# Two-layer S5 and attention decoder on one core: sums of squares on TensorE column parts in layer 0, and new engines and step orders

## The chip, the cores and the metric

One core of a Trainium2 chip runs the whole program. The metric is device microseconds of one execution, lower is better. Engines are called as the profile calls them: PE (TensorE), DVE (VectorE), ACT (ScalarE), POOL (GpSimd), SP (the queue that issues the loads).

## The reference

The input is x (256 tokens by 1024) and 256 memory tokens. There are two layers. Cut to what matters:

```python
for l in range(2):
    h = rms_norm(x, ln_mix[l]); z = h @ w_in[l]
    u_self, q_mem = z[..., :768], z[..., 768:]
    if l == 0: self_out = s5_mixer(u_self, ...)      # scan over tokens, gelu, gate
    else:      self_out = causal attention of rope(u_self) with keys, values of rms_norm(x) @ w_kv
    mem_out = memory_attention(q_mem, mem, mem_norm[l], w_mem_kv[l])   # 4 heads
    x = x + concat([self_out, mem_out]) @ w_out[l]
    x = x + conv_ffn(x, ...)
return rms_norm(x, final_norm)

def rms_norm(x, gain):
    return x * rsqrt(mean(x * x, axis=-1) + 1e-6) * gain
```

What the change touches is the mean of x * x of the input and of the memory in layer 0, the operators of the S5 mixer, and the copies of keys for attention.

## The kernel before, in words

Activations lie with features on the 128 partitions and tokens along the free dimension. Weights stream from HBM through one SP queue in the order of use. The program has five stages, one behind the other: the mixer of layer 0 (about the first 170 us), its feed-forward part, the mixer of layer 1 (from about 360 to 480 us), its feed-forward part, and the final norm.

**Norms.** The scale of a token is not applied to the input of a projection but to its output. ACT squares x into four tiles of 128x512 (`squares`, L275). `sums` (L279) adds the four on POOL in three instructions (L280 to L282) and then lets PE add over partitions: four products, each with a 128x128 part of the sum as the stationary operand and a column of ones as the moving one (L286), so that the sum of token n lands on partition n. An f32 product shows as two instructions in the trace. `root` (L290) makes the reciprocal root with a few 128x2 DVE instructions (L293, L301 to L305) and one POOL power (L299). `spread` (L312) brings the result to all partitions through PE, and ACT copies it to `rb` (L1015). In layer 0 the steps are called rx1 (sums), rx2 (root), rx3 (spread and copy) for x, and rm0 (squares), rm1, rm2, rm3 for the memory.

**Mixer of layer 0.** Its order is written out by hand in the string ORDER (L43): each word is a step, and the instructions of PE, DVE and POOL keep the order of the steps up to the bar, while ACT and SP are ordered by the compiler's planner. Behind the bar the string only sets priorities, and the planner orders all engines. The steps: P (one half block of the input projection, 8 PE instructions at L866; `project`, L860), u (DVE product of a projection block with rb, L874, which is the first use of rb), U (places u for the scan, ACT or DVE, L883, L885), E (powers for the rotation, L782, on DVE at L642 or on POOL at L639), X (input operators, two products and two sums of 512 elements, L751), T and t (PE transposes of X at L775 and their copies), V (output operators, three instructions of 1024 elements, L808), l and L (local operator, PE products on 32-column parts at L834 and L838, ACT copies at L849), S (the states, four parts: PE products at L895, a rotation of six DVE instructions at L902 to L907, two scans at L910 and L911, eight DVE instructions at L916 to L925), Y (outputs: PE at L939 and L943, a copy yc at L949 or L951, transposes, a copy yT at L959 or L961), G (gelu), K and K1 (memory keys and values of layers 0 and 1: eight PE steps, then the product kT at L392 and the copies `stack_k`), q (memory queries), h (a head in four parts), p (a pair of heads), g and o (gate, output projection), z (residual). Tuples beside ORDER say which of these parts run on which engine: V_POOL, X_POOL, E_POOL, Y_ACT, EVAC_ACT.

**Key copies.** `stack_k` (L415) makes, for each half of 64 partitions, a rounded copy on ACT (L421), the same copy into the other half on POOL (L422) and the remainder by a subtraction (L423), on POOL for the memory keys. `stack_q` (L406) does likewise with one copy and one subtraction.

**Mixer of layer 1.** ORDER1 (L61) lists its steps; here the string only sets priorities for the planner. ST_DVE names the stacks whose subtraction runs on DVE.

Of the kernel before, what the change touches and what calls it, by code (L numbers as in the profile page):

```python
# [10 lines left out]
F32 = mybir.dt.float32  # L11
# [31 lines left out]
ORDER = """  # L43
P E0 P P E1 P P P rm0 E0 Xr0 rx1 P P P rx2 E0 rx3 E0 E1 P Xi0 u0 D0 P U0 T0 U0 P U0 t0 P E1 D2 Xr1 P U0 V0 B0 Xi1 S0
u1 V0 V0 l0 T1 Xi2 U1 S0 P U1 S0 l0 V2 V1 P V1 L0 V2 t1 K Xr2 B1 S0 L0 T2 U1 K u2 V1 rm1 U2 K U2 U1 L0 L0 Y0 B2 K U2
t2 U2 E1 S1 V2 l1 D1 l1 l1 l1 L1 rm2 L1 S1 rm3 S2 Y0 S1 S1 K L1 K S2 K S2 Y0 L1 S2 K K1 Y1 K G0 G0 | q Y2 Y2 h1 Y1 h2
Y1 h1 h3 h3 K1 K1 h0 Y2 h2 G1 h1 G2 h0 K1 K1 h0 K1 G1 h2 G2 h3 h1 h2 h0 K1 h3 K1 g g g g g p1 g0 g0 g g1 p0 g1 p1 K1
g2 p0 o o o o g2 o o o o z3 z2 z1 z0
"""
V_POOL = ((2, 2),)  # L50
X_POOL = ((2, 0),)
E_POOL = ((0, 3), (1, 0), (1, 1), (1, 2))
H_DVE = (0, 1, 2)
Y_ACT = (1,)
EVAC_ACT = (0, 2)
T_ACT = ((0, 0), (0, 1), (1, 1), (2, 0), (2, 1))
# [4 lines left out]
ORDER1 = """  # L61
x x x x I I I X r1 r2 I I I I r3 I X Q0 qm Q1 K K Q1 h0 K X h3 X h2 Q2 K h1 h0 K h2 h2 R0 h1 h2 v Q0 R1 v R0 h3 R1 v
h0 h3 h1 K Q2 h10 h7 h0 h1 h5 v R2 h4 h3 h5 h4 h4 h7 v v h8 h5 h4 h11 h6 h10 h9 v v p0 h6 e0 h9 h10 h6 R2 h13 h5 p1 h7
h8 h14 h8 h7 h8 h12 h6 p1 p0 e1 h10 h9 h12 O h11 p3 h13 h12 h12 h9 h15 h11 p3 h13 h14 h11 h15 h14 p4 p5 h13 h15 p2 p2
p5 p4 p6 O h14 O h15 p7 p6 p7 O z0 O O O O z3 z2 z1
"""
ST_DVE = (('k', 1), ('q', 0))
BANKS = 'aaarwa'
# [71 lines left out]
def _body(ctx, tc, a):  # L140
# [138 lines left out]
    def sums(ts, bk):  # L279
# [8 lines left out]
        return p  # L288

    def root(p):  # L290

        m = sm.tile([128, 2], F32, name="m")
        V.tensor_scalar(m, p[:, :2], 1.0 / D, EPS, op0=ALU.mult, op1=ALU.add)  # L293
        return newton(m, 2)
# [83 lines left out]
    def mem_kv(l, bk, mem, ks, new, vm):  # L378
# [13 lines left out]
        V.tensor_mul(kT, v2(pk), rb2(rbm))  # L392
        ks.extend(stack_k(kT, new, G))
        for t in range(2):
# [10 lines left out]

    def stack_q(src, new, eng):  # L406

        n = src.shape[1]
        t = [new([128, n, T], F32R, "qs") for _ in range(2)]
        for h in range(2):  # L410
            S.activation(t[h][HALF[h]], src[HALF[h]], AF.Copy)
            eng.tensor_sub(t[h][HALF[1 - h]], src[HALF[h]], t[h][HALF[h]].bitcast(F32))
        return t

    def stack_k(src, new, eng):  # L415

        n = src.shape[1]
        t = [new([128, n, T], F32R, "ks") for _ in range(4)]
        for h in range(2):
            G.memset(t[2 + h][HALF[1 - h]].bitcast(F32), 0.0)  # L420
            S.activation(t[h][HALF[h]], src[HALF[h]], AF.Copy)  # L421
            G.tensor_copy(t[h][HALF[1 - h]], src[HALF[h]])  # L422
            eng.tensor_sub(t[2 + h][HALF[h]], src[HALF[h]], t[h][HALF[h]].bitcast(F32))  # L423
        return t
# [170 lines left out]
    def layer0(pool, s5):  # L595
# [412 lines left out]
        def rx1():  # L1008
            d["px"] = sums(xsq, bw)

# [9 lines left out]
        def rm1():  # L1020
            d["pm"] = sums(d["sm"], ba)

# [34 lines left out]
        def q():  # L1057
            qm = sq([128, 2, T], name="qm")
            V.tensor_mul(qm, v2(acc[3]), rb2(rb))
            qs.extend(stack_q(qm, st, V))  # L1060

# [32 lines left out]
    def layer1(pool):  # L1094
# [33 lines left out]
        def mem_q():  # L1128
            t = sl([128, 2, T], name="qm")
            V.tensor_mul(t, v2(d["q"][3]), rb2(rb))  # L1130
            qm.extend(stack_q(t, st, V if "qm" in ST_DVE else G))

        def rope(name, b, stack, out):
# [9 lines left out]
            yield  # L1143
            out[b] = stack(t, st, V if (name, b) in ST_DVE else G)
            yield
# [138 lines left out]
```

## Time and profile before

| what | value |
|---|---|
| median of 3 runs | 671.42 us (670.06 to 672.51) |
| the profiled execution's own time | 671.97 us |
| its span | 670.2 us |
| mean granted clock of PE | 0.966 of full speed |
| chain that ended last, by engine | PE 76%, DVE 18%, ACT 2%, issue 2% |

The span lies 1.8 us under the execution's own time. In a timeline each row is a start, a length, an engine, a line and an operation; several equal ones in a row are merged (x3), and the length then runs from the first start to the last end. What stands in brackets is the idle time of the engine before it and what ended it. In a table of stretches each engine has its busy time and, in brackets, its instructions; PEclk is the granted clock, where 1.00 is 2.4 GHz and 0.50 is 1.2 GHz.

### The profile page before, as it was taken

To read this page: it belongs to the slowest core of one execution; us is meant where nothing else is said; L and a number is where in the kernel's file an instruction comes from. 1 tells how busy PE (TensorE), PEld (TensorE's weight loads), DVE (VectorE), ACT (ScalarE), POOL (GpSimd) and SP (SyncE) were. 2 spreads that over 40 slices of the span, in tenths; PEclk is the share of its full clock that TensorE was granted. 3 is DMA by queue.
4 is the path that set the end of the run, shared out by engine and by line. 5 is a ranking of instruction groups with operands and counts; after the bars stand their busy time and mean duration, and the time that the engine had idled before them with its cause. 6 is when DMAs were issued, how large, how long until landed. Compare 5 with 4: busy or idle time off the path is not lost.

```text
span 670.2 us, 12678 instructions
## 1 busy us (share of the span) xinstructions
PE 629.2 (94%) x4968; PEld 595.2 (89%) x4968; DVE 547.5 (82%) x1011; ACT 408.0 (61%) x746; POOL 103.7 (15%) x117
## 2 busy tenths in 40 slices
PE   6787597999999999999999998999999999999995
PEld 5676586899999999999999997879999999999984
DVE  7989899786699988787769799875479998888872
ACT  5597454675566556565548788774446665555641
POOL 4596303031200000000003226301200000000000
PEclk9799698899999999999999997999999999999998
DMA  8722313256457436455465142424345555555511
GB/s 301 253 96 63 104 48 119 95 190 220 155 191 251 169 117 236 157 205 188 149 237 173 65 166 99 150 73 165 109 138 189 193 183 186 186 188 189 189 33 63
DMA packets 43356, 105.24 MB, mean 157 GB/s; under 512 B 3744, under 2 KB 14240, under 8 KB 43296
## 3 DMA queue, kind: packets, MB, share of 16 engines
q1 hardware_dynamic: 42720, 103.84, 45.6%
q8 instruction: 39, 0.64, 0.4%
q10 hardware_dynamic: 576, 0.59, 0.3%
q14 instruction: 21, 0.17, 0.1%
HBM read 103.37 MB, written 1.05 MB: 156 GB/s over the span
## 4 chain that ended last, share of the span: by engine, by line
PE 76%; DVE 18%; ACT 2%; issue 2%; DMA 0%; POOL 0%; DVEq 0%; ACTq 0%
PE psU L262 13%; PE psU L260 12%; PE psU L261 12%; PE acc L562 9%; PE acc L261 7%; PE acc L262 7%; PE acc L260 7%; DVE wlo L119 2%; DVE X L642 1%; PE psO L481 1%; DVE xt L642 1%; PE ps L388 1%; DVE cf L649 1%; DVE Vd L642 1%; PE psT L465 1%
## 5 line engine op out<-in xcount | busy, mean ns | idle before, releaser
L115 ACT ACTIVATE whi<-wraw 128x1024 fp32r<-128x1024 f32 (+1 forms) x176 | 181.1, 1037 | 102.7 <-PE psU L261 52.0
L119 DVE TENSOR_TENSOR wlo<-wraw,whi 128x1024 fp32r<-128x1024 f32 (+1 forms) x176 | 212.8, 1212 | 31.2 <-PE psU L262 14.9
L262 PE MATMUL psU<-xhi,wlo 128*128 128x256 f32 x704 | 197.6, 281 | 1.1 <-DVE wlo L119 1.1
L260 PE MATMUL psU<-xhi,whi 128*128 128x256 f32 x704 | 198.0, 282 | 0.0
L261 PE MATMUL psU<-xlo,whi 128*128 128x256 f32 x704 | 197.4, 281 | 0.0
L262 PEld LDWEIGHTS psU<-xhi,wlo 128*128 128x128 f32 x704 | 133.2, 189 | 1.4 <-DVE wlo L119 1.3
L261 PEld LDWEIGHTS psU<-xlo,whi 128*128 128x128 f32 x704 | 132.6, 189 | 0.7
L260 PEld LDWEIGHTS psU<-xhi,whi 128*128 128x128 f32 x704 | 132.4, 188 | 0.7
L533 DVE SCALAR_TENSOR_TENSOR y<-u,held,y 128x254 f32<-128x254 f32 (+1 forms) x176 | 77.9, 477 | 1.5 <-ACT y L531 1.3
L531 ACT ACTIVATE y<-u,held 128x256 f32<-128x256 f32 x88 | 47.7, 590 | 20.6 <-DVE u L526 20.6
L526 DVE TENSOR_TENSOR u<-psU,rb 128x512 f32<-128x512 f32 x44 | 30.3, 688 | 33.3 <-PE psU L262 33.1
L261 PE MATMUL acc<-al,whi 128*128 128x256 f32 x176 | 49.6, 282 | 0.0
L260 PE MATMUL acc<-ah,whi 128*128 128x256 f32 x176 | 49.6, 282 | 0.0
L262 PE MATMUL acc<-ah,wlo 128*128 128x256 f32 x176 | 49.6, 282 | 0.0
L280 POOL TENSOR_TENSOR sq<-sq 128x512 f32<-128x512 f32 x5 | 8.2, 1648 | 229.7 <-ACT sq L275 229.7
L866 PE MATMUL acc<-xg,wraw 128*128 128x256 f32 x128 | 34.5, 431 | 5.5 <-ACT xg L856 5.5
L866 PEld LDWEIGHTS acc<-xg,wraw 128*128 128x128 f32 x128 | 27.8, 222 | 10.0 <-ACT xg L856 5.5
L262 PEld LDWEIGHTS acc<-ah,wlo 128*128 128x128 f32 x176 | 33.6, 191 | 0.0
L261 PEld LDWEIGHTS acc<-al,whi 128*128 128x128 f32 x176 | 33.6, 191 | 0.0
L260 PEld LDWEIGHTS acc<-ah,whi 128*128 128x128 f32 x176 | 33.5, 190 | 0.0
L262 PE MATMUL acc<-xhi,wlo 128*128 128x256 f32 x112 | 31.6, 283 | 0.0
L261 PE MATMUL acc<-xlo,whi 128*128 128x256 f32 x112 | 31.4, 281 | 0.0
(253 smaller groups left out, 1322.8 us busy)
## 6 DMA issues: line engine op xcount, KB each, us to landing
wraw<-w_up SPq DMA_DIRECT2D x88, 512.0 KB, 4.2
wraw<-w_down SPq DMA_DIRECT2D x44, 512.0 KB, 4.0
wraw<-w_out SPq DMA_DIRECT2D x16, 512.0 KB, 3.6
wraw<-w_in SPq DMA_DIRECT2D x15, 512.0 KB, 5.7
wraw<-w_mem_kv SPq DMA_DIRECT2D x8, 512.0 KB, 3.8
wraw<-w_kv SPq DMA_DIRECT2D x6, 512.0 KB, 7.4
wraw<-w_kv SPq DMA_DIRECT2D x8, 384.0 KB, 3.4
wraw<-w_glu SPq DMA_DIRECT2D x6, 384.0 KB, 3.7
```

Of the source, the lines that this page charges most:

```text
L115: self.nc.scalar.activation(hi[:, c], t[:, c], AF.Copy, scale=1.0 if g_ is None else g_)
L119: self.nc.vector.tensor_sub(lo[:, c], t[:, c], hi[:, c].bitcast(F32))
L260: PE.matmul(out, whi, ahi, start=first, stop=False, skip_group_check=True)
L261: PE.matmul(out, whi, alo, start=False, stop=False, skip_group_check=True)
L262: PE.matmul(out, wlo, ahi, start=False, stop=last, skip_group_check=True)
L280: G.tensor_add(ts[0], ts[0], ts[1])
L526: V.tensor_mul(u, v2(p), rb2(rb))
L531: S.activation(y[:, j], u[:, j], AF.Identity, bias=cp(3), scale=cp(2))
L533: V.scalar_tensor_tensor(y[:, j, d:], u[:, j, :T - d], cp(2 - d), y[:, j, d:], op0=ALU.mult, op1=ALU.add)
L562: PE.matmul(dacc[2 * t + h], a_, w_[:, 512 * i:512 * i + 512], start=False, stop=last and a_ is al, skip_group_check=True)
L642: V.tensor_tensor(o, a_, b_, op=op)
L866: PE.matmul(acc[2 * h + b][:, 256 * (m % 2):256 * (m % 2) + 256], w[:, 512 * i + 128 * m:512 * i + 128 * m + 128], xg[k // 2][:, k % 2], s ...
```

## The change

- `sums_pe` replaces `sums` at rx1 and rm1, both in layer 0. There is no addition on POOL; PE takes each of the four tiles of squares as stationary operand in parts of 32 columns, each on its own 32 columns of the array, and accumulates: 64 products with one moving column in place of four. The norms of the feed-forward parts and of layer 1 keep `sums`.
- V_POOL: the last sum of V2 goes from POOL to DVE. E_POOL: the second part of E0 goes from DVE to POOL, the first part of E1 from POOL to DVE.
- Y_ACT: yT of block 2 goes from DVE to ACT. EVAC_ACT: yc of block 1 goes to ACT and that of block 2 to DVE.
- CP_ACT: the second key copy of both memory stacks (names m0, m1) goes from POOL (L422) to ACT. The engines of all subtractions stay as they are; they only get other names.
- ORDER and ORDER1 list the same steps in another order.

```diff
@@ -41,30 +41,31 @@
 ENG = mybir.EngineType
 MANUAL = {ENG.PE, ENG.DVE, ENG.Pool}
 ORDER = """
-P E0 P P E1 P P P rm0 E0 Xr0 rx1 P P P rx2 E0 rx3 E0 E1 P Xi0 u0 D0 P U0 T0 U0 P U0 t0 P E1 D2 Xr1 P U0 V0 B0 Xi1 S0
-u1 V0 V0 l0 T1 Xi2 U1 S0 P U1 S0 l0 V2 V1 P V1 L0 V2 t1 K Xr2 B1 S0 L0 T2 U1 K u2 V1 rm1 U2 K U2 U1 L0 L0 Y0 B2 K U2
-t2 U2 E1 S1 V2 l1 D1 l1 l1 l1 L1 rm2 L1 S1 rm3 S2 Y0 S1 S1 K L1 K S2 K S2 Y0 L1 S2 K K1 Y1 K G0 G0 | q Y2 Y2 h1 Y1 h2
-Y1 h1 h3 h3 K1 K1 h0 Y2 h2 G1 h1 G2 h0 K1 K1 h0 K1 G1 h2 G2 h3 h1 h2 h0 K1 h3 K1 g g g g g p1 g0 g0 g g1 p0 g1 p1 K1
-g2 p0 o o o o g2 o o o o z3 z2 z1 z0
+P E0 rm0 E0 P P P Xr0 P P rx1 E1 E0 V0 P P P P rx2 P rx3 E0 D0 P u0 Xi0 U0 E1 t0 Xi1 V0 P B0 U0 E1 U0 P U0 T0 P u1 V1
+Xr1 S0 V0 T1 l0 V2 U1 S0 P V1 l0 V2 Xi2 K K L0 S0 Xr2 L0 u2 D1 U1 S0 L0 t1 L0 T2 U1 K U2 t2 rm1 U2 Y0 V2 B2 B1 U1 K V1
+D2 rm2 S1 Y0 U2 E1 l1 l1 l1 U2 S1 K l1 rm3 S2 K L1 S1 S2 L1 K L1 Y0 S1 K G0 S2 S2 K1 K L1 | Y1 Y2 q K1 K1 Y1 Y1 h2 h1
+K1 h1 G1 h3 K1 h3 h1 h1 G0 Y2 Y2 h2 G1 K1 G2 h2 K1 G2 g h0 h0 g h0 g h3 g h2 g0 h0 g h3 g1 p0 K1 g0 K1 o o g g2 g1 g2
+p0 o p1 o p1 o o z0 o o z1 z3 z2
 """
-V_POOL = ((2, 2),)
+V_POOL = ()
 X_POOL = ((2, 0),)
-E_POOL = ((0, 3), (1, 0), (1, 1), (1, 2))
+E_POOL = ((0, 1), (0, 3), (1, 1), (1, 2))
 H_DVE = (0, 1, 2)
-Y_ACT = (1,)
-EVAC_ACT = (0, 2)
+Y_ACT = (1, 2)
+EVAC_ACT = (0, 1)
 T_ACT = ((0, 0), (0, 1), (1, 1), (2, 0), (2, 1))
 U_ACT = ((1, 1, 1, 0), (1, 1, 1, 1), (1, 1, 1, 1))
 
 
 
 ORDER1 = """
-x x x x I I I X r1 r2 I I I I r3 I X Q0 qm Q1 K K Q1 h0 K X h3 X h2 Q2 K h1 h0 K h2 h2 R0 h1 h2 v Q0 R1 v R0 h3 R1 v
-h0 h3 h1 K Q2 h10 h7 h0 h1 h5 v R2 h4 h3 h5 h4 h4 h7 v v h8 h5 h4 h11 h6 h10 h9 v v p0 h6 e0 h9 h10 h6 R2 h13 h5 p1 h7
-h8 h14 h8 h7 h8 h12 h6 p1 p0 e1 h10 h9 h12 O h11 p3 h13 h12 h12 h9 h15 h11 p3 h13 h14 h11 h15 h14 p4 p5 h13 h15 p2 p2
-p5 p4 p6 O h14 O h15 p7 p6 p7 O z0 O O O O z3 z2 z1
+x x x x I I I X r1 r2 I I I I r3 I X Q0 qm K Q1 K Q1 Q2 h0 K X h3 X h2 K h1 h0 K h2 h2 R0 h1 h2 v Q0 R1 R0 h3 R1 v v
+h0 h3 h1 K Q2 h10 h7 h0 h1 h5 v R2 h4 h3 h5 h4 h4 h7 v v p0 h8 h5 h4 h11 h6 h10 v p0 h6 e0 h9 h10 h6 R2 h13 h8 h5 p1
+h7 h14 h9 v h8 h7 h8 h12 h6 p1 e1 h10 h9 h12 O h11 p3 h13 h12 h12 h9 h15 h11 p3 h13 h14 h11 h15 h14 p4 p5 h13 h15 p2
+p2 p5 p4 p6 O h14 O h15 p7 p6 p7 O O z0 O O O z3 z2 z1
 """
-ST_DVE = (('k', 1), ('q', 0))
+ST_DVE = ('k1', 'q0', 'w0')
+CP_ACT = ('m0', 'm1')
 BANKS = 'aaarwa'
 
 
@@ -287,6 +288,17 @@
                           start=(h == 0), stop=(h == 1))
         return p
 
+    def sums_pe(ts, bk):
+
+        p = bk()
+        for t in range(2):
+            for i, (q, h) in enumerate((q, h) for q in ts for h in range(2)):
+                for c in range(4):
+                    n = 256 * h + 128 * t + 32 * c
+                    PE.matmul(p[32 * c:32 * c + 32, t:t + 1], q[:, n:n + 32], ones, start=i == 0,
+                              stop=i == 2 * len(ts) - 1, tile_position=(0, 32 * c), skip_group_check=True)
+        return p
+
     def root(p):
 
         m = sm.tile([128, 2], F32, name="m")
@@ -390,7 +402,7 @@
             yield
         kT = sq([128, 2, NM], name="kT")
         V.tensor_mul(kT, v2(pk), rb2(rbm))
-        ks.extend(stack_k(kT, new, G))
+        ks.extend(stack_k(kT, new, f"m{l}"))
         for t in range(2):
             S.activation(vm[:, t], pv[:, 256 * t:256 * t + 256], AF.Copy, scale=rtok[:, t:t + 1])
         yield
@@ -403,24 +415,30 @@
     def values_of(v):
         return lambda h: [v[:, t, 64 * h:64 * h + 64] for t in range(2)]
 
-    def stack_q(src, new, eng):
+    def less(name, out, src, hi):
+        (V if name in ST_DVE else G).tensor_sub(out, src, hi.bitcast(F32))
+
+    def stack_q(src, new, name):
 
         n = src.shape[1]
         t = [new([128, n, T], F32R, "qs") for _ in range(2)]
         for h in range(2):
             S.activation(t[h][HALF[h]], src[HALF[h]], AF.Copy)
-            eng.tensor_sub(t[h][HALF[1 - h]], src[HALF[h]], t[h][HALF[h]].bitcast(F32))
+            less(name, t[h][HALF[1 - h]], src[HALF[h]], t[h][HALF[h]])
         return t
 
-    def stack_k(src, new, eng):
+    def stack_k(src, new, name):
 
         n = src.shape[1]
         t = [new([128, n, T], F32R, "ks") for _ in range(4)]
         for h in range(2):
             G.memset(t[2 + h][HALF[1 - h]].bitcast(F32), 0.0)
             S.activation(t[h][HALF[h]], src[HALF[h]], AF.Copy)
-            G.tensor_copy(t[h][HALF[1 - h]], src[HALF[h]])
-            eng.tensor_sub(t[2 + h][HALF[h]], src[HALF[h]], t[h][HALF[h]].bitcast(F32))
+            if name in CP_ACT:
+                S.activation(t[h][HALF[1 - h]], src[HALF[h]], AF.Copy)
+            else:
+                G.tensor_copy(t[h][HALF[1 - h]], src[HALF[h]])
+            less(name, t[2 + h][HALF[h]], src[HALF[h]], t[h][HALF[h]])
         return t
 
     def scores(bk, q, k, i, h, causal):
@@ -1006,7 +1024,7 @@
             gens[f"G{b}"] = gelu2(b)
 
         def rx1():
-            d["px"] = sums(xsq, bw)
+            d["px"] = sums_pe(xsq, bw)
 
         def rx2():
             d["yx"] = root(d["px"])
@@ -1018,7 +1036,7 @@
             d["sm"] = squares([m.rearrange("p a t -> p (a t)") for m in memT])
 
         def rm1():
-            d["pm"] = sums(d["sm"], ba)
+            d["pm"] = sums_pe(d["sm"], ba)
 
         def rm2():
             d["ym"] = root(d["pm"])
@@ -1057,7 +1075,7 @@
         def q():
             qm = sq([128, 2, T], name="qm")
             V.tensor_mul(qm, v2(acc[3]), rb2(rb))
-            qs.extend(stack_q(qm, st, V))
+            qs.extend(stack_q(qm, st, "w0"))
 
         calls = {"rx1": rx1, "rx2": rx2, "rx3": rx3, "rm0": rm0, "rm1": rm1, "rm2": rm2, "rm3": rm3, "q": q}
         for b in range(3):
@@ -1128,7 +1146,7 @@
         def mem_q():
             t = sl([128, 2, T], name="qm")
             V.tensor_mul(t, v2(d["q"][3]), rb2(rb))
-            qm.extend(stack_q(t, st, V if "qm" in ST_DVE else G))
+            qm.extend(stack_q(t, st, "w1"))
 
         def rope(name, b, stack, out):
             sw = sl([128, 2, T], name="sw")
@@ -1141,7 +1159,7 @@
             V.tensor_mul(sw, sw, rb2(ropeS))
             V.tensor_add(t, t, sw)
             yield
-            out[b] = stack(t, st, V if (name, b) in ST_DVE else G)
+            out[b] = stack(t, st, f"{name}{b}")
             yield
 
         def keys():
```

## Rows read from the trace of the kernel before

**Rows 1.** The page's part 1: busy time, share of the span, instructions.

```profile
PE 629.2 (94%) x4968; PEld 595.2 (89%) x4968; DVE 547.5 (82%) x1011; ACT 408.0 (61%) x746; POOL 103.7 (15%) x117
```

**Rows 2.** Busy time by stretch: columns PE, PEld, DVE, ACT, POOL, PEclk, DMA share, GB/s.

```profile
20.00:30.00 10.00, 8.14 (x29) 7.12 (x30) 8.84 (x41) 7.90 (x18) 2.56 (x4) 0.66 0.69 245
60.00:70.00 10.00, 3.26 (x20) 2.53 (x20) 10.00 (x9) 2.90 (x5) 4.32 (x3) 0.92 0.17 52
...
140.00:150.00 10.00, 10.00 (x83) 8.68 (x82) 8.02 (x12) 6.93 (x11) 5.40 (x4) 1.00 0.56 186
410.00:420.00 10.00, 8.98 (x40) 8.42 (x40) 9.32 (x19) 7.84 (x17) 3.73 (x3) 0.50 0.50 168
```

**Rows 3.** Timeline of POOL, first 110 us: start, length, instruction, [idle before].

```profile
17.91 1.29 POOL L280 TENSOR_TENSOR sq<-sq 128x512 f32<-128x512 f32 x1
...
55.93 1.49 POOL L280 TENSOR_TENSOR sq<-sq 128x512 f32<-128x512 f32 x1
...
66.91 2.35 POOL L639 TENSOR_TENSOR Vd<-Vd,vt 128x1024 f32<-128x1024 f32 x1 [5.68 <-DVE vt L642]
...
107.11 0.74 POOL L422 CAST ks<-kT 64x512 fp32r<-64x512 f32 x1 [25.41 <-DVE kT L392]
```

**Rows 4.** Timeline of DVE up to the first product with rb (L874).

```profile
17.99 1.25 DVE L746 TENSOR_TENSOR s5c<-cf 128x24 f32<-128x24 f32 x1
...
19.26 2.73 DVE L731 TENSOR_TENSOR ct<-s5c 128x48 f32<-128x48 f32 x4
...
22.82 0.64 DVE L731 TENSOR_TENSOR ct<-s5c 128x72 f32<-128x72 f32 x3
...
29.95 1.31 DVE L642 TENSOR_TENSOR xt<-s5c 128x512 f32<-128x512 f32 x2
31.30 2.04 DVE L642 TENSOR_TENSOR X<-xt 64x512 f32<-64x512 f32 x2
34.11 0.69 DVE L874 TENSOR_TENSOR uT<-acc,rb 128x512 f32<-128x512 f32 x1 [0.78 <-ACT rb L1015]
```

**Rows 5.** Timeline of PE: first sums, projection steps, local operator, first scores.

```profile
21.86 1.86 PE L286 MATMUL ps<-held,sq 128*128 128x1 f32 x8 [3.35 <-POOL sq L282]
23.58 7.29 PE L866 MATMUL acc<-xg,wraw 128*128 128x256 f32 x24
...
31.16 3.62 PE L866 MATMUL acc<-xg,wraw 128*128 128x256 f32 x16
...
47.05 0.43 PE L834 MATMUL ps<-Vd,Bz 128*32 128x64 f32 x16 [2.73 <-DVE Vd L642]
...
113.45 0.77 PE L431 MATMUL psS<-ks,qs 128*128 128x256 f32 x2 [3.03 <-DVE qs L412]
```

**Rows 6.** Timeline of ACT: the copy of rb.

```profile
33.70 0.38 ACT L1015 ACTIVATE rb<-ps 128x256 f32<-128x256 f32 x1
```

**Rows 7.** Timeline of DVE behind it, to the memory keys (L392).

```profile
48.37 0.69 DVE L780 COPY RT<-ps 128x512 f32<-128x512 f32 x1 [1.46 <-PE ps L775]
...
55.61 0.68 DVE L906 TENSOR_TENSOR rot<-rot 128x512 f32<-128x512 f32 x1
56.21 1.76 DVE L907 TENSOR_TENSOR rot<-rot 128x512 f32<-128x512 f32 x1
57.89 2.28 DVE L910 TENSOR_TENSOR_SCAN rot<-dec,rot 128x512 f32<-128x512 f32 x1
...
67.36 2.45 DVE L916 TENSOR_TENSOR rot<-rot,E 128x512 f32<-128x512 f32 x1
...
74.96 1.22 DVE L642 TENSOR_TENSOR Vd<-Vd,vt 128x1024 f32<-128x1024 f32 x1
...
82.75 0.69 DVE L902 TENSOR_TENSOR rot<-ps,E 128x512 f32<-128x512 f32 x1 [1.16 <-PE ps L895]
...
86.42 1.22 DVE L910 TENSOR_TENSOR_SCAN rot<-dec,rot 128x512 f32<-128x512 f32 x1
...
106.36 0.68 DVE L392 TENSOR_TENSOR kT<-ps,held 128x512 f32<-128x512 f32 x1
```

## The prediction

> **What bounds the kernel now.** I read the page's busy times first [rows 1]: PE is busy 94% of the span and DVE 82%, so most of the program is PE's, and only a stage where PE waits can give time back. The table of stretches says which stages these are [rows 2]. From 140 us on PE is full for as long as the mixer and the feed-forward part last; whatever moves the start of that stage moves the end one to one. Before it PE is short of work: 3.26 us of 10 between 60 and 70, while DVE has its full 10, and between 20 and 30 PE also runs at a granted clock of 0.66, a mean of its two levels. So the first 106 us, up to the product kT, are a DVE queue whose order is written by hand, and a change is worth there what it takes from that queue. In the mixer of layer 1 one stretch stands out, 410 to 420, where PE is busy for 8.98 us at half clock; little else is open there.
>
> The timelines of POOL and DVE, laid side by side, show where the queue loses time. While POOL adds squares [rows 3], DVE instructions on two SBUF operands take about one POOL instruction longer [rows 4, 7]: the 24-column L746 took 1.25 us, four L731 took 2.73 us where three later ones took 0.64, the scan L910 took 2.28 us at 57.89 and 1.22 at 86.42. This hold is the first thing the change removes.
>
> **Part by part, up to u0.** *rx1.* The PE timeline shows PE idle for 3.35 us ahead of the four old products [rows 5], waiting for POOL's third addition; PE was thus free at 21.86 - 3.35 = 18.5. The new products need only the squares from ACT, so they start there. There are 64, or 128 instructions. Their price is not in the trace. The nearest row is L834, also 32 stationary columns on a column part, 16 instructions in 0.43 us, 27 ns each. The far bound is that a part costs what a whole product costs: L286, eight in 1.86 us at about half clock, 232 ns, so 116 ns at full clock. Below 27 ns I see no reason to go. I take 27, because width and part are the same, and keep 116 for the rivals: 128 x 27 ns = 3.45 us, until 22.0.
>
> The Trainium skill has a rule against it: "TensorE: Matmul & The Clock Gate", section "Wait — 56ns, not 53.3ns?", says that small products have floors of their own, about 25 ns from start to start, or about 62 ns where the sequencer's microcode handles each. The row of L834 agrees with the first floor. By the second, rx1 would last 7.9 us and the sum below would come out 4.5 us later.
>
> *rx3 and u0.* Between rx1 and rx3 the new order has five P steps where the old one had three. A step is 8 instructions, 3.62 / 16 x 8 = 1.81 us at full clock [rows 5], so 9.05 us. Behind its pause PE took 7.29 us for three steps instead of 5.43: 1.86 us lost to the clock. The pause goes; whether the clock falls during rx1 all the same, no row shows. Bounds 0 and 1.86; I take 0.9. So the spread starts at 22.0 + 9.05 + 0.9 = 31.9 and with 0.6 for it and 0.4 for ACT's copy u0 starts at 33.0 (32.0 to 34.0). Before it was 34.11 [rows 4]. The copy stood at 33.70 [rows 6] behind work that waited for Xi0; in the new order Xi0 comes behind u0, so nothing of it can stand ahead of the copy.
>
> *The wait that this makes.* DVE used to do Xi0 while rb was coming. In the new order nothing of DVE stands between rx2 and u0. DVE ended Xi0 at 31.30 + 2.04 = 33.34. Off that come the hold on L746 and L731 (1.25 - 0.21 and 2.73 - 4 x 0.21, together 2.9) and Xi0 itself (33.34 - 29.95 = 3.4); on come 1.2 for the first product of V0, which moves ahead. E0's second part leaves DVE and E1's first part comes to it, ten small instructions for eight; I cost the swap at nothing, within 0.3 us either way. DVE is ready at 28.3 and waits 4.7 us for rb, with the whole queue behind it. So the 2.9 us of rx are nearly all given back here, and u0 gains 1.1 us.
>
> **From u0 to kT.** Before, this was 106.36 - 34.11 = 72.25 us [rows 4, 7]. The terms:
> - rm1 without POOL: L907 took 1.76 us against 0.68 of L906, the scan 2.28 against 1.22, and I take the same again for the second scan: -3.2.
> - V2's sum to DVE: POOL's 2.35 us go, which held L916 for 2.45 instead of 0.68; the sum costs DVE 1.22, as V1's did: -1.77 + 1.22 = -0.55.
> - DVE's old idle, 1.46 ahead of RT and 1.16 ahead of L902: -2.6. The wait for POOL's power in rm2 stays.
> - Xi0 now lies behind u0, 1.31 + 2 x 0.68 = +2.7 without POOL beside it; V0's first product has left: -1.2.
> - rm1's 128 instructions on PE, 3.45 us, cost nothing as long as they run while PE waits for the states of block 0; that stretch had 6.7 us of idle PE in ten [rows 2].
> - New waits of DVE in the new order: U0, T1, S1 and S2 all come on PE shortly ahead of their use. At least 0, at most about 5, twice the old idle; I take 2.0.
> - Xr2 stays on POOL, but now falls beside more instructions on two SBUF operands. Between 0 and 3.5 (one hold of 1.06 to 1.77 for two or three more); I take 1.0.
>
> Sum: 72.25 - 3.2 - 0.55 - 2.6 + 2.7 - 1.2 + 2.0 + 1.0 = 70.4. kT starts at 33.0 + 70.4 = 103.4, 3.0 us earlier.
>
> **Behind kT.** Both POOL copies of the keys (0.74 us for the first [rows 3]) go to ACT, which then has six copies in line where it had four; POOL's subtractions come earlier, the queries' copies later. PE waited 3.03 us for the first scores [rows 5]. Between 0.7 lost and 1.5 won; I take 0.8. yT of block 2 leaves DVE, about 0.6 as for other 512-element copies [rows 7]; the swap of yc is one for one and costs nothing unless PE waits for it, 0.7 at most. Together 1.4. The second memory stack runs while PE is full and gives nothing.
>
> **Layer 1.** ORDER1 is only a priority for the planner, and no engine changes. All that is open is the half-clock stretch [rows 2], where full clock would give back up to 4.5 us; a worse order could make another such stretch. I take 0, within 2 either way.
>
> **Sum.** 3.0 + 1.4 = 4.4 us off the profiled execution's 671.97, so 667.6. That execution stands 0.55 above the median of the runs shown; against the median I forecast 667.0.
>
> **The rivals.**
> *More is won.* The stall at u0 is short because rx1 keeps PE's clock, the queue behind finds its PE results ready, and layer 1 gets back its half-clock stretch. Forecast less 1.0 (u0), 2.0 (waits), 2.5 of layer 1: about 661. For it: 2.9 + 3.2 + 1.77 us of holds are measured. Against it: the DVE wait at u0 is in the order itself. Chance 0.17.
> *No change.* Small products at the skill's second floor, or waits at their upper bound: by either, +4.5 or +3 and Xr2's +2.5, 670 to 672.5. For it: PE is idle for 6.7 us of one stretch of ten [rows 2] and the new order moves nearly every step, so a hold can come back as a wait for PE. Against it: 27 ns in the trace. Chance 0.18.
> *Slower: the column parts do not overlap.* All 64 products add to two columns, each part to the same place every fourth time; if one has to wait for another, rx1 takes up to 128 x 116 ns = 14.8 us, u0 starts at 44.4 and the end is 11.4 us later than forecast, 678.4. It decides from about 80 ns per instruction, 10.2 us for rx1, which is 6.7 more than I take and 2 us above the time before. For it: no row has one moving column on a column part. Against it: L834 accumulates too and shows 27 ns. Chance 0.12.
>
> **How the numbers follow.** The forecast has 0.53. Its own range, with u0 by 1 us, waits by 2.0 down and 3 up, Xr2, the keys and layer 1 at their bounds but not all at once, is 663 to 670. For 8 in 10 I reach to the middle of the two outer cases, 660 to 673. About 0.3%, 2 us, is what a measurement of this kernel can tell from no change. Faster by more (below 669.4): 0.17 and nearly all of 0.53, 0.67. Within it: 0.18. Slower: 0.15, the last rival and a part of the second.
>
> **What would show it.** In the new profile: no L280 on POOL in layer 0; L746 and L731 at some 0.2 us; L910 at 1.2 us each time; 128 short PE instructions from about 18.5 us, lasting some 3.5 us; an idle DVE of 3 to 6 us ahead of L874, ended by ACT's rb; kT at 102 to 104 us. The sum is wrong if u0 starts later than 36, if DVE is idle for more than 5 us between u0 and kT, or if the layer 1 mixer changes by over 2 us.

## The result, and the profile after

The changed kernel takes 660.56 us (median of 4 runs, 660.06 to 661.47) against 670.74 us for the kernel before (4 runs beside it, 669.62 to 672.51): a ratio of 0.9844, 95% interval 0.9819 to 0.9869. It is 10.2 us faster; the profiled span fell by 11.1, from 670.2 to 659.1. The forecast was 667.0 us, 4.4 us faster: the direction was right and the time lies in the range of 660 to 673, at its very end, but more than twice the forecast was won. The profile of the kernel before is of an execution of 671.97 us, 1.2 above this median, so the stretches below overstate the gain by about 1 us.

I cut both profiles at the same places: u0 (the first product with rb), kT, the first memory scores, the first product of the gate, the first sums over partitions of the feed-forward part of layer 0 (ffn0), the same of layer 1's mixer and feed-forward part, and the end of the span. Start times and differences in us:

| stretch | before | after | change | forecast |
|---|---|---|---|---|
| start to u0 | 34.11 | 30.96 | -3.15 | -1.1 |
| u0 to kT | 72.25 | 71.18 | -1.07 | -1.85 |
| kT to scores | 7.09 | 7.67 | +0.58 | |
| scores to gate | 10.66 | 3.86 | -6.80 | kT to gate: -1.4 |
| gate to ffn0 | 50.42 | 50.48 | +0.06 | 0 |
| ffn0 to sums of layer 1's mixer | 191.02 | 191.51 | +0.49 | 0 |
| these to sums of layer 1's feed-forward part | 112.85 | 113.01 | +0.16 | 0 |
| these to the end of the span | 191.80 | 190.43 | -1.37 | 0 |

The page of the kernel after (its first line and part 1) shows 5.3 us less PE time than [rows 1], at a mean granted clock of 0.980 for 0.966, and 11 us less on POOL:

```profile
span 659.1 us, 13141 instructions
PE 623.9 (95%) x5208; PEld 589.8 (89%) x5208; DVE 541.0 (82%) x1009; ACT 411.6 (62%) x751; POOL 92.4 (14%) x108
```

Stretches of the kernel after, with the columns of [rows 2]:

```profile
20.00:30.00 10.00, 8.36 (x41) 7.10 (x40) 8.01 (x32) 6.59 (x17) 4.76 (x14) 1.00 1.05 375
60.00:70.00 10.00, 8.74 (x199) 7.52 (x200) 9.86 (x14) 8.10 (x24) 0.00 (x0) 0.84 0.01 3
110.00:120.00 10.00, 10.00 (x71) 9.82 (x71) 8.48 (x21) 5.41 (x15) 0.00 (x0) 0.83 0.44 157
400.00:410.00 10.00, 8.02 (x38) 7.47 (x39) 9.32 (x17) 8.06 (x16) 4.22 (x3) 0.55 0.50 165
```

One of these stretches was not among the rows of before; there it reads:

```profile
110.00:120.00 10.00, 6.30 (x27) 5.61 (x27) 9.69 (x13) 6.30 (x13) 2.63 (x3) 0.64 0.55 197
```

PE keeps its full clock between 20 and 30 us, where it had 0.66, and between 110 and 120 it is busy all the time (at a granted clock of 0.83), where it was busy for 6.30 at 0.64. The slow stretch of layer 1's mixer is still there, only some 10 us earlier.

PE up to u0, to set beside [rows 5]:

```profile
17.58 1.27 PE L298 MATMUL ps<-held,sq 128*32 128x1 f32 x128
18.78 8.90 PE L884 MATMUL acc<-xg,wraw 128*128 128x256 f32 x40
29.33 0.71 PE L324 MATMUL ps<-held,y 128*128 128x128 f32 x4 [1.64 <-DVE y L317]
```

The 128 new instructions take 1.27 us, 10 ns each. The five P steps behind them take 8.90 us, 1.78 each (2.43 before). PE is ready for the spread at 27.7 and then waits for DVE's y. DVE in the same time and just behind, to set beside [rows 4]:

```profile
18.61 0.18 DVE L764 TENSOR_TENSOR s5c<-cf 128x24 f32<-128x24 f32 x1
...
18.84 0.56 DVE L749 TENSOR_TENSOR ct<-s5c 128x48 f32<-128x48 f32 x4
...
26.55 1.22 DVE L660 TENSOR_TENSOR Vd<-s5c 128x1024 f32<-128x1024 f32 x1
27.68 0.15 DVE L305 TENSOR_SCALAR m<-ps 128x2 f32<-128x2 f32 x1
28.66 0.16 DVE L313 TENSOR_TENSOR t<-y 128x2 f32<-128x2 f32 x1 [0.82 <-POOL y L311]
...
30.96 0.69 DVE L892 TENSOR_TENSOR uT<-acc,rb 128x512 f32<-128x512 f32 x1 [1.69 <-ACT rb L1033]
31.57 1.62 DVE L660 TENSOR_TENSOR xt<-s5c 128x512 f32<-128x512 f32 x2
```

L764 and L749 are L746 and L731 of before: 0.18 for 1.25 us and 0.56 for 2.73. The root (from L305) stands behind the first product of V0. Further down the same queue, to kT:

```profile
47.46 0.69 DVE L798 COPY RT<-ps 128x512 f32<-128x512 f32 x1 [0.42 <-PE ps L793]
...
51.60 1.51 DVE L924 TENSOR_TENSOR rot<-rot 128x512 f32<-128x512 f32 x1
53.03 1.76 DVE L925 TENSOR_TENSOR rot<-rot 128x512 f32<-128x512 f32 x1
...
59.73 1.23 DVE L928 TENSOR_TENSOR_SCAN rot<-dec,rot 128x512 f32<-128x512 f32 x1
...
98.44 0.68 DVE L996 TENSOR_TENSOR yl<-yT,yh 128x512 fp32r<-128x512 f32 x1
...
102.14 0.68 DVE L404 TENSOR_TENSOR kT<-ps,held 128x512 f32<-128x512 f32 x1
```

The scan takes 1.23 (L910 took 2.28), and between u0 and kT DVE waits only for 0.42 us for PE and 0.83 for POOL's power. L924 and L925 are held by Xr2 on POOL (1.51 and 1.76 for 0.68), whose second half is this row:

```profile
51.30 2.94 POOL L657 TENSOR_TENSOR X<-xt 64x512 f32<-64x512 f32 x2
```

L996 ends the gelu work of block 0, which now lies ahead of kT.

PE behind kT, first before (between these lines stand the scores of [rows 5]), then after:

```profile
107.13 3.29 PE L388 MATMUL ps<-wraw,memT 128*128 128x256 f32 x14
...
119.64 4.83 PE L388 MATMUL ps<-wraw,memT 128*128 128x256 f32 x14
124.11 0.47 PE L260 MATMUL acc<-yh,whi 128*128 128x256 f32 x1
```

```profile
104.14 1.13 PE L397 MATMUL ps<-memT,wraw 128*128 128x256 f32 x4
105.11 1.03 PE L400 MATMUL ps<-wraw,memT 128*128 128x256 f32 x4
109.81 0.39 PE L449 MATMUL psS<-ks,qs 128*128 128x256 f32 x1 [3.68 <-DVE qs L419]
...
113.67 0.56 PE L261 MATMUL acc<-yh,whi 128*128 128x256 f32 x1
```

Before, 28 instructions of K1's values (second memory projection) follow kT, 14 of them behind the scores and ahead of the gate. After, nine follow kT, eight of them in the two rows shown (each group of four is two products), and none the scores. Scores to gate lost 6.8 us: 4.5 are these 14 instructions (119.64 to 124.11), 0.9 a group of PE transposes that no longer stands there, 0.7 a wait for yc that is gone, and 0.7 faster scores. From kT to the gate that is 6.2 us, where I had forecast 1.4.

### The profile page after: what moved, and what is told of

Its sections match the earlier page's. It is cut to its first block, busy times and chain, and to the rows that moved or that the text cites. A ratio compares the mean times of both kernels' runs of the same rounds, so it can differ in the third digit from the quotient of the medians.

```text
span 659.1 us, 13141 instructions
## 1 busy us (share of the span) xinstructions
PE 623.9 (95%) x5208; PEld 589.8 (89%) x5208; DVE 541.0 (82%) x1009; ACT 411.6 (62%) x751; POOL 92.4 (14%) x108
## 4 chain that ended last, share of the span: by engine, by line
PE 75%; DVE 3%; ACT 1%; issue 1%; DVEq 0%; POOL 0%; POOLq 0%
PE psU L263 13%; PE psU L261 13%; PE psU L262 13%; PE acc L580 9%; PE acc L262 7%; PE acc L263 7%; PE acc L261 7%; PE psO L499 1%; DVE wlo L120 1%; PE psS L449 1%; PE psT L483 1%; PE psS L450 1%; PE acc L538 1%; PE acc L1181 1%; PE acc L1182 0%
## 5 line engine op out<-in xcount | busy, mean ns | idle before, releaser
L120 DVE TENSOR_TENSOR wlo<-wraw,whi 128x1024 fp32r<-128x1024 f32 (+1 forms) x176 | 216.7, 1234 | 16.7 <-PE acc L263 8.1
L281 POOL TENSOR_TENSOR sq<-sq 128x512 f32<-128x512 f32 x3 | 4.8, 1598 | 233.7 <-DMA wraw<-w_kv 178.1
L884 PE MATMUL acc<-xg,wraw 128*128 128x256 f32 x128 | 32.0, 411 | 5.6 <-ACT xg L874 5.6
L884 PEld LDWEIGHTS acc<-xg,wraw 128*128 128x128 f32 x128 | 26.0, 207 | 9.6 <-ACT xg L874 5.6
```

The source lines that it names most:

```text
L120: self.nc.vector.tensor_sub(lo[:, c], t[:, c], hi[:, c].bitcast(F32))
L884: PE.matmul(acc[2 * h + b][:, 256 * (m % 2):256 * (m % 2) + 256], w[:, 512 * i + 128 * m:512 * i + 128 * m + 128], xg[k // 2][:, k % 2], s ...
```

## The experiments

Theory: the gain is the end of POOL's hold on DVE, plus PE work that no longer stands behind the scores. Rivals: the new orders and engines bring it and the sums matter little; or DVE and PE had been waiting for the sums, and POOL's hold matters little. Times are medians; each ratio is to the kernel before on the same chip. Cuts are start times of one profile each.

| kernel | us | ratio (95%) | u0 | kT | scores | gate | ffn0 |
|---|---|---|---|---|---|---|---|
| old_plus_sums | 663.56 | 0.9898 (0.9878 to 0.9918) | 31.23 | 101.34 | 108.43 | 116.24 | 166.66 |
| new_pool_sums | 673.28 | 1.0038 (1.0025 to 1.0052) | 40.23 | 111.43 | 119.10 | 123.39 | 174.49 |
| new_old_order | 663.03 | 0.9888 (0.9872 to 0.9903) | 31.29 | 99.75 | 106.49 | 116.77 | 167.22 |
| old_rx_only | 668.10 | 0.9968 (0.9955 to 0.9981) | 31.25 | 104.74 | 111.83 | 119.64 | 170.06 |
| old_rm_only | 666.65 | 0.9949 (0.9927 to 0.9972) | | | | | |
| old_sums_idle_adds | 666.62 | 0.9940 (0.9919 to 0.9961) | 31.15 | 105.10 | 112.18 | 120.00 | 170.51 |
| early_root | 660.93 | 0.9866 (0.9831 to 0.9900) | 29.27 | 102.18 | 109.95 | 113.58 | 163.88 |
| new_old_tail | 668.17 | 0.9959 (0.9943 to 0.9976) | 31.20 | 103.02 | 111.41 | 115.70 | 172.09 |
| old_hand_k1 | 665.47 | 0.9916 (0.9888 to 0.9944) | 31.52 | 105.69 | 114.42 | 118.73 | 170.28 |
| old_sums_k1front | 666.38 | 0.9939 (0.9918 to 0.9961) | 31.40 | 102.01 | 114.06 | 119.17 | 170.27 |
| k1_behind | 676.43 | 1.0088 (1.0058 to 1.0117) | 30.76 | 106.39 | 111.64 | 115.90 | 180.34 |
| new_pool_copies | 665.68 | 0.9928 (0.9900 to 0.9956) | 31.12 | 102.29 | 110.48 | 113.46 | 167.98 |
| new_m0_dve | 658.16 | 0.9810 (0.9781 to 0.9840) | 30.81 | 102.02 | 108.86 | 112.46 | 162.00 |
| new_old_order1 | 663.11 | 0.9882 (0.9852 to 0.9913) | 30.83 | 102.00 | 109.66 | 113.52 | 164.12 |
| early_root_m0 | 659.66 | 0.9832 (0.9801 to 0.9862) | 28.98 | 101.96 | 108.89 | 113.15 | 163.60 |
| after_again | 661.12 | 0.9860 (0.9834 to 0.9886) | 30.74 | 102.78 | 110.45 | 114.73 | 165.37 |

The last row is the changed kernel once more. Its start times differ from the first profile's by up to 1.2 us, so smaller differences of start times between kernels are not read; stretches repeat better (kT to scores is 7.67 us in both, scores to gate 3.86 and 4.28, gate to ffn0 50.48 and 50.64).

**The new sums alone (old_plus_sums).** The kernel before with `sums_pe` added and nothing else:

```diff
-            d["px"] = sums(xsq, bw)
+            d["px"] = sums_pe(xsq, bw)
-            d["pm"] = sums(d["sm"], ba)
+            d["pm"] = sums_pe(d["sm"], ba)
```

> The kernel before, with the sums of x and of the memory in layer 0 taken by TensorE on column parts, and nothing else changed. Theory A (hand order: of the 10.2 us, about 6 come from behind kT, because the new hand-written part lets the planner put the second memory stack's products ahead of the first scores; the holds of DVE by POOL's additions give the rest): the holds go, u0 starts 2.5 to 3.5 us earlier and kT 5 to 6 us earlier, but 14 value products of the second stack still stand between the scores and the first gate product; 664 to 666.5 us. Theory B (holds: the additions on POOL were all that mattered, and the rest followed from an earlier DVE): 660 to 662 us.

Measured 663.56, between the two ranges: 7.5 of the 10.2 us (by the ratio 6.8, between 5.5 and 8.2). kT comes 5.0 us earlier, and kT to gate falls from 17.75 to 14.90 although PE's order there is that of before. Its PE timeline:

```profile
102.50 3.29 PE L399 MATMUL ps<-wraw,memT 128*128 128x256 f32 x14
108.43 0.48 PE L442 MATMUL psS<-ks,qs 128*128 128x256 f32 x2 [2.63 <-DVE qs L423]
...
113.41 3.19 PE L399 MATMUL ps<-wraw,memT 128*128 128x256 f32 x14
116.24 0.47 PE L260 MATMUL acc<-yh,whi 128*128 128x256 f32 x1
```

The same 14 instructions that took 4.83 us take 3.19: this stretch keeps the full clock (granted 1.00 between 110 and 120, 0.64 before). Why the clock differs is not shown, and the shorter wait ahead of the scores does not explain it: behind the same wait (2.64 us) the scores of old_rx_only run slowly (granted 0.83 between 110 and 120) and the 14 instructions take 3.19 again.

**The rest without the new sums (new_pool_sums).** The changed kernel with `sums` back at both places, the same diff reversed.

> The changed kernel with both sums of layer 0 back on POOL (three additions, four products). Theory A: the products of the second memory stack stay ahead of the scores, and only the two holds come back, 2 x 3 us less what the wait ahead of u0 covers: 664 to 667 us. Theory B: nearly all of the gain is lost, 668 to 671 us.

It is slower than the kernel before, by 2.2 us, and above both ranges. DVE and PE in its first 42 us:

```profile
40.23 0.69 DVE L892 TENSOR_TENSOR uT<-acc,rb 128x512 f32<-128x512 f32 x1 [9.09 <-ACT rb L1033]
```

```profile
28.06 11.27 PE L884 MATMUL acc<-xg,wraw 128*128 128x256 f32 x40
39.16 0.61 PE L324 MATMUL ps<-held,y 128*128 128x128 f32 x4
```

PE adds over partitions only at 26.34, as POOL's additions start later in the new order (at 21.93, before at 17.91), and the five P steps of 11.27 us still stand between that and the spread of the root. In the new order u0 has nothing between it and rx2, so all this stops the whole DVE queue: u0 is 9.3 us later than in the changed kernel, kT also 9.3. So the new ORDER needs the fast sums: with them it wins (next run), without them the rest of the change loses. The parts don't add up.

**The new engines in the old order (new_old_order).** The changed kernel with all of ORDER from before; ORDER1, CP_ACT and the other tuples stay.

> The changed kernel with the whole old string ORDER (hand part and tail), the new engines and sums kept. Theory A: a little better than the old kernel with new sums alone, 662.5 to 666 us, with products of the second memory stack still behind the first scores. Theory B: 660 to 662 us, as the changed kernel.

663.03 is the time of the sums alone (the intervals overlap). So the engines and ORDER1 give nothing beside the sums as long as ORDER is the old one, and the new ORDER gives the last 2.5 us.

**One of the two norms (old_rx_only, old_rm_only).** The first line of the first diff alone, and the second alone.

> The kernel before with only the sums of x on TensorE. Both theories: u0 earlier by about 2.9 us (31.2) and u0 to kT as before, about 72 us, so kT at 103.4; 667 to 669 us. If the two sums add up, this gain and that of the memory's sums together are the 7.5 us of both; if what follows kT (TensorE's clock, the wait ahead of the first scores) has a threshold, they add to less or more.

> The kernel before with only the memory's sums on TensorE (x keeps POOL's additions). Hold theory (a POOL addition beside DVE delays DVE's instructions on two SBUF operands by about its own length, and nothing waits for this sum itself): DVE's queue wins 3.2 us between u0 and kT, u0 stays at 34; 666.5 to 668.5 us. Wait theory (what counts is that a consumer had waited for POOL's result): nothing waited for rm1, so no change, 670 to 672 us.

0.32% and 0.51%: both win, and together they give the 1.02% of old_plus_sums within the intervals. For old_rm_only only the time was read. The profile of old_rx_only ends 4.1 us ahead of that of the kernel before (its kT is 1.6 earlier, its gate 4.5), where its ratio is worth 2.1 us (1.3 to 3.0). So some of what the profiles show between kT and gate, 14.90 us for 17.75 here too, is the profiled execution of the kernel before and not won in every one.

**Hold or wait (old_sums_idle_adds).** old_plus_sums with three additions on POOL whose results nobody reads:

```diff
+            u = [sm.tile([128, 512], F32, name=f"un{i}", bufs=1) for i in range(3)]
+            for i in range(3):
+                G.tensor_add(u[i], d["sm"][i], d["sm"][i + 1])
             d["pm"] = sums_pe(d["sm"], ba)
```

> The kernel before with both sums on TensorE, and three additions of 512 elements on POOL at the memory's sums, whose results nobody reads. Hold theory: the additions alone bring back 2 to 3.5 us: 665.5 to 667.5 us, with DVE instructions of twice their length beside them. Wait theory: 663 to 664.5 us, as without them.

It loses about 3 us against old_plus_sums (0.0042 of the ratio is 2.8, the medians differ by 3.1), and kT comes 3.8 us later. POOL, and DVE beside it:

```profile
54.05 5.25 POOL L1034 TENSOR_TENSOR un<-sq 128x512 f32<-128x512 f32 x3
```

```profile
54.26 1.76 DVE L918 TENSOR_TENSOR rot<-rot 128x512 f32<-128x512 f32 x1
55.94 2.29 DVE L921 TENSOR_TENSOR_SCAN rot<-dec,rot 128x512 f32<-128x512 f32 x1
58.16 2.22 DVE L922 TENSOR_TENSOR_SCAN rot<-dec,rot 128x512 f32<-128x512 f32 x1
```

The first two in old_plus_sums (the third takes 1.19 there):

```profile
54.34 0.68 DVE L918 TENSOR_TENSOR rot<-rot 128x512 f32<-128x512 f32 x1
54.94 1.21 DVE L921 TENSOR_TENSOR_SCAN rot<-dec,rot 128x512 f32<-128x512 f32 x1
```

Nobody waits for these additions, and still each DVE instruction takes 1.03 to 1.08 us longer. This shows the hold, and for rm1 it rules out that a wait for the sums was the cause.

**The stall at u0 (early_root).** The changed kernel with rx2 ahead of E1, E0 and V0, so that nothing of DVE delays the root:

```diff
-rx1 E1 E0 V0 P P P P rx2 P rx3 E0 D0 P u0 Xi0
+rx1 P P P rx2 E1 P rx3 E0 V0 P E0 D0 P u0 Xi0
```

> The changed kernel with the root of x (rx2) ahead of E1, E0 and V0 on DVE, and the spread one projection step earlier. If the 1.69 us of DVE's wait ahead of u0 pass through: u0 at 29.0 to 30.0 and 658.5 to 659.8 us. If another wait takes their place: 660 to 661 us.

u0 comes 1.7 us earlier and the idle time of DVE is gone, but kT stays where it was and the time is the same. The first two DVE instructions of Xi0 show where it went:

```profile
29.88 2.45 DVE L660 TENSOR_TENSOR xt<-s5c 128x512 f32<-128x512 f32 x2
```

The pair took 1.62 in the changed kernel: POOL's powers of E0, a part of which ran while DVE waited for rb, now run beside Xi0 and Xi1 and hold them. Between u0 and kT this and smaller holds cost 1.0 us; the other 0.7 went to a longer wait for PE ahead of RT (1.12 us for 0.42).

**Hand-written part or tail (new_old_tail).** The changed kernel with the words behind the bar from before, and Y1 and G0 in front of them, which the old hand-written part had held.

> The changed kernel with the old words behind the bar of ORDER (with the two steps Y1 and G0 that the new hand part leaves over put in front). Theory A: what counts is the hand part, so 659.5 to 662 us. Rival C (the tail's priorities, K1 named earlier, made the gain behind kT): 665 to 668 us.

668.17 lies just above the rival's range. Scores to gate stays short (4.3 us), so that comes from the new hand-written part. But gate to ffn0 takes 56.4 us instead of 50.5. Two stretches of this kernel, then of the changed one:

```profile
120.00:130.00 10.00, 8.79 (x67) 6.95 (x66) 6.72 (x17) 8.23 (x18) 2.24 (x2) 1.00 0.03 6
130.00:140.00 10.00, 6.77 (x54) 6.36 (x54) 9.32 (x11) 8.59 (x12) 0.99 (x1) 1.00 0.75 252
```

```profile
120.00:130.00 10.00, 9.36 (x74) 8.10 (x74) 9.04 (x17) 9.46 (x21) 0.00 (x0) 1.00 0.56 165
130.00:140.00 10.00, 10.00 (x85) 9.33 (x84) 8.86 (x11) 8.01 (x13) 3.90 (x2) 1.00 0.57 193
```

The old tail leaves PE short of work just behind the gate's start. So the new hand-written part with the old tail is 5.1 us slower than the old order altogether (new_old_order): the new hand-written part wins only with a tail that suits it.

**K1 ahead of the scores in the old order.** Two tries: seven K1 words of the tail written into the hand-written part of the kernel with new engines and old order (old_hand_k1), and all eight first behind the bar of old_plus_sums, for the planner to place (old_sums_k1front).

```diff
-S2 K K1 Y1 K G0 G0 | ...
+S2 K K1 K1 K1 Y1 K1 K1 K1 K1 K1 K G0 G0 | ...
```

> New engines and sums with the old order, and in its hand part seven more steps K1 (products of the second memory stack) ahead of the bar, so that none is left behind the first scores. If the place of these products is what the new order wins behind kT: first gate product 4 to 5 us after the first scores in place of 10.3, kT at 100 to 101, 657 to 660 us. If they only push other products back: 661.5 to 664 us, as with the old order.

```diff
-S2 K K1 Y1 K G0 G0 | q Y2 Y2 h1 ...
+S2 K K1 Y1 K G0 G0 | K1 K1 K1 K1 K1 K1 K1 K1 q Y2 Y2 h1 ...
```

> The kernel before with the new sums and the eight K1 steps first behind the bar; the compiler's planner then takes K1's products while PE waits ahead of the scores. Theory (the place of K1's products makes the stretch behind kT short): the 14 products that stood between scores and gate (3.19 us) leave that place, scores to gate falls from 7.8 to 4.0 to 4.6 us, kT stays within 0.5 us, and the time falls by 2 to 3.5 us, to 660 to 661.5. Rival (that stretch is short because of block 0's gelu, 2.5 us of DVE that the new order moves ahead of kT): DVE ends the wait for the first gate product, which starts less than 1 us earlier, 663 to 664.

Both miss. Scores to gate falls as meant (4.3 and 5.1 us), and as much is lost ahead of it: old_hand_k1 has kT 5.9 us later, old_sums_k1front the scores 5.0 us later behind kT. PE of the second:

```profile
99.80 6.31 PE L399 MATMUL ps<-wraw,memT 128*128 128x256 f32 x28
114.06 0.55 PE L442 MATMUL psS<-ks,qs 128*128 128x256 f32 x1 [5.99 <-ACT held L406]
```

and POOL, ahead of that wait's end:

```profile
108.58 1.98 POOL L433 CAST ks<-kT 64x512 fp32r<-64x512 f32 x2
110.64 3.54 POOL L434 TENSOR_TENSOR ks<-kT,ks 64x512 fp32r<-64x512 f32 x2
```

Here the products bring their followers with them: layer 1's kT, its copies on POOL (which hold DVE) and the value copies on ACT, for which the scores then wait. In old_hand_k1 it is other work: against new_old_order DVE has three more weight remainders ahead of kT (2.7 us) and is idle for 3.5 us more, 2.5 of them in one wait for ACT's whi.

**K1 behind the gate's start (k1_behind).** The changed kernel with all nine K1 words ahead of the first G2. The planner puts 32 products (64 instructions) behind the start of the gate.

```diff
-... S2 S2 K1 K L1 | Y1 Y2 q K1 K1 Y1 ...
+... S2 S2 K L1 | Y1 Y2 q Y1 Y1 h2 h1 h1 G1 h3 h3 h1 h1 G0 Y2 Y2 h2 G1 K1 K1 K1 K1 K1 K1 K1 K1 K1 G2 ...
```

> The changed kernel with all steps of K1 behind the gelu of the blocks, so that the planner puts 32 products of the second memory projection (64 instructions of 0.215 us, 13.8 us) behind the start of the gate. Theory (those products cost nothing ahead of the scores, where PE waits, and their whole length behind them): gate starts at 113 to 114 as in the changed kernel, the sums of the feed-forward part come 10 to 14 us later, 671 to 674. Rival (PE has room behind the gate too, or the order only shifts waits): less than 4 us later, 661 to 665.

15.9 us slower than the changed kernel. Gate to ffn0 grows from 50.5 to 64.4, by 14.0 us, against the 13.8 expected. (The time lies above its range, as the gate itself starts 2.2 us later.) Most of it lies in two rows:

```profile
121.01 4.91 PE L397 MATMUL ps<-memT,wraw 128*128 128x256 f32 x22
125.76 5.34 PE L400 MATMUL ps<-wraw,memT 128*128 128x256 f32 x24
```

So a product of K1 costs its whole length behind the gate's start. (That kT is also 4.3 us later is DVE's: the planner fills the queue ahead of it with five weight remainders.)

**Key copies (new_pool_copies).** The changed kernel with `CP_ACT = ()`.

> The changed kernel with the key copies back on POOL. If they matter as the prediction took it (0.8 us, first scores earlier): first scores 0.5 to 1.5 us later, 661 to 662.5 us. If the chain of ACT or of DVE's held subtraction sets the scores anyway: 660 to 661 us.

The time is above both ranges. The scores come 0.5 us later behind kT, where I had forecast 0.8, and 5.1 us are lost in all, 4 of them between gate and ffn0, where the planner orders the tail otherwise. So this run does not price the copies alone; the 0.5 us ahead of the scores are all that can be put down to them.

**First memory keys' subtractions on DVE (new_m0_dve).** The changed kernel, with

```diff
-ST_DVE = ('k1', 'q0', 'w0')
+ST_DVE = ('k1', 'q0', 'w0', 'm0')
```

> The changed kernel with the subtractions of the first memory keys (m0) on DVE in place of POOL. POOL's two subtractions held four DVE instructions (wlo) for 5.7 us where they take 3.6 alone; if that hold delays the queries and the scores, the scores come 1 to 2 us earlier and the time is 658.5 to 660 us. If the four instructions and two more on DVE cost as much: 660 to 661.5 us.

658.16, the fastest of all: 0.9810 against 0.9844 and 0.9860 for the changed kernel, the intervals overlapping at their ends, its slowest run (659.63) below the fastest of theirs (660.06). DVE in the changed kernel, POOL beside it, and DVE here:

```profile
103.33 5.70 DVE L120 TENSOR_TENSOR wlo<-wraw,whi 128x768 fp32r<-128x768 f32 x4
```

```profile
103.56 1.84 POOL L419 TENSOR_TENSOR ks<-kT,ks 64x512 fp32r<-64x512 f32 x1 [29.38 <-ACT ks L436]
```

```profile
103.22 3.56 DVE L120 TENSOR_TENSOR wlo<-wraw,whi 128x768 fp32r<-128x768 f32 x4
106.69 1.40 DVE L419 TENSOR_TENSOR ks<-kT,ks 64x512 fp32r<-64x512 f32 x2
```

The two subtractions cost DVE 1.40 us and free it of 2.14 us of hold; the scores come 6.84 us behind kT instead of 7.67.

**The rest.** new_old_order1 is the changed kernel with the old ORDER1; early_root_m0 joins early_root and new_m0_dve; after_again has no edit.

> The changed kernel with the old order of layer 1. The traces show the stretch between the sums of layer 1 and those of its feed-forward part at 112.85 us before and 113.01 after, so no gain there: 659.5 to 661.5 us. If ORDER1 brought the 0.7 us that the end wins over it: 661 to 662 us.

> The early root of x together with the first memory keys' subtractions on DVE. If the early root gives nothing whatever stands behind it, the time is that of the subtractions alone, 657.5 to 659; if its 1.7 us at u0 were only held up by POOL behind kT, it is 656 to 657.

> The changed kernel once more, beside these: 660 to 661.5; milestones within 0.2 us of those of its first profile as far as kT.

The old ORDER1 leaves layer 1's mixer where it was (113.40 us between its sums and those of the feed-forward part, 113.01 after, 112.85 before); its ratio overlaps the changed kernel's. Its median is still 2.5 us above that kernel's and above both ranges; the profile has 0.4 us of this in the mixer and 1.1 behind the sums of the feed-forward part, so it is not excluded that ORDER1 is worth some 2 us in the new order. early_root_m0, at 659.66, is above both its ranges: the early root gives nothing here either.

## Why the prediction was right and wrong

**Right: the holds, the stages, the direction.** The holds that the sum counted are gone row by row, and old_sums_idle_adds shows that they were holds. From the gate's start to layer 1's feed-forward part the start moved the end one to one, within 0.7 us. "Layer 1: 0 within 2" held: 0.16 us. The rival of slower column parts is out. Of the end, 1.4 us more came off behind that; 0.8 of it is idle PE between 480 and 490 that is no longer there (8.86 us busy before, 9.63 in the stretch that answers to it); the other 0.6 was not followed.

**Wrong by 2.05 us: u0.** "27 ns is taken" for the new products; they took 10 ns, 1.27 us for 3.45, below the lower end of my bounds. The 27 ns of L834 are a mean: in its trace four column parts start 6 to 10 ns apart, with 31 to 35 ns between most groups of four. The clock stayed at its upper level (I took 0.9 us of loss), rx1 started at 17.58 and not at 18.5, and PE was ready at 27.7, not 31.9. The limit then passed to DVE's root behind V0's first product, and u0 started at 30.96, not 33.0; the wait of DVE for rb was 1.69 us, not 4.7. Two signs that I had named, 3.5 us of short instructions and 3 to 6 us of idle DVE, did not appear. The rule that the prediction set beside the row, floors of 25 or 62 ns for small products (the Trainium skill, "TensorE: Matmul & The Clock Gate", section "Wait — 56ns, not 53.3ns?"), does not hold for these: by its lower floor rx1 would have taken 3.2 us.

**Right in sum, wrong in terms: u0 to kT.** 71.18 us against 70.4. Not foreseen: 2.5 us of block 0's gelu (L988 to L996, 0.43 + 0.69 + 0.68 + 0.68) came ahead of kT, because the new hand-written part has G0 there. POOL's powers and other holds made the products and sums of X and V cost about 0.5 us more than counted. Against these, new waits were 0.42 us, not 2.0, and Xr2's hold mostly moved: it lengthens L924 and L925 by 1.9 us now, but before it had lengthened two products of X at 50.29 by 1.5 (2.89 for 1.4), so it cost 0.4 more and not 1.0. That the errors cancel to 0.8 is luck. u0 and this together put kT at 102.14, 1.3 us earlier than forecast and inside the named 102 to 104.

**The step that failed: "behind kT".** I costed key copies and yT there, 1.4 us, and let everything else shift one to one. It fell by 6.2 us. I had shown the wait for the scores, and not read what PE does between scores and gate: 14 instructions of K1, 4.83 us at a low clock, which nothing ahead of the gate needs. So I let the stretch shift as a block, and put the new order's effect on it at nothing. Shown by runs: with the sums alone the profile has 14.90 us from kT to gate for 17.75, the 14 instructions at full clock (how much of this each execution of the kernel before loses is open); the new hand-written part takes the products away from there (4.3 us from scores to gate even with the old tail); and their price behind the gate's start is their whole length (k1_behind). Moving them alone gives nothing in the old order, since other work then delays kT or the scores. Which words of the new hand-written part keep that work away was not tried, nor why single words of the tail move gate to ffn0 between 50.4 and 56.4 us; that stays open.

**Where the 10.2 us are.** 7.5 by the sums alone, about 0.5 (not to be told from nothing) by the engines and ORDER1 added to them, the last 2.5 by ORDER (by the ratios 6.8, 0.7 and 3.0), and without the sums all the rest together costs 2.2. My rival "more is won, 661" had the right number and two of its three reasons, the short stall and the missing waits, but not layer 1; the number is luck all the same, for the gelu ahead of kT took back most of what these two gave, and the 4.8 us beyond forecast behind kT are none of its reasons.

## What to carry to other kernels

Work on a second engine can hold the busy one: three additions that took POOL 5.25 us and that nobody read cost DVE 3.2. Look for rows of one operation with two durations, and at what runs beside the longer; adding such idle work measures the price. When a start moves, don't let the stretch behind it shift as a block: list what the bound engine does there that nobody waits for yet, because that is what a new order can pull into earlier gaps. An order tuned to a fast step can be slower than the old one without it, so undo the step inside the new order too.

## What was not expected of the hardware

- Products with 32 stationary columns and one moving column, on four column parts in turn, took 10 ns each (128 in 1.27 and in 1.25 us), where the same width with 64 moving columns took 27 ns [rows 5].
- The same 14 instructions in the same order ran in 3.19 us instead of 4.83, at a granted clock of 1.00 for 0.64 in that stretch; the wait ahead of the scores, 2.63 us for 3.03, hardly differed.
- With the wait at u0 removed, POOL's powers slid beside DVE's products (two of them 2.45 us for 1.62), and the holds took back 1.0 of the 1.7 us: an idle stretch of DVE had been the cover for part of POOL's work.
